# Norm weights applied by feature after the transposes, the stream transposed unweighted, scatter products split in two, first products in other PSUM banks

## The chip, the cores and the metric

The kernel runs on one core of a Trainium2 chip. The metric is device time in microseconds (us) of one execution. Five engines work side by side, each through its own instructions in a fixed order: PE (TensorE, matrix products and transposes), DVE (VectorE), ACT (ScalarE), POOL (GpSimd) and SP, which here only issues DMAs. An instruction that waits for another engine holds up everything behind it on its own engine. Before the change the kernel takes 1525.91 us, the median of three runs (1525.18 to 1528.49).

## The reference

256 tokens of 1024 features run through two blocks. Cut to what matters here, every sublayer reads a normalised copy of the stream `h` and adds its result back; in the second block the result is normalised too:

```
def rms_norm(x, gain):
    y = x * rsqrt(mean(x * x, axis=-1) + EPS)
    return y * gain

mem_n = rms_norm(mem, mem_norm)
h = x
h = h + hybrid_mixer(rms_norm(h, mix_norm), ...)
h = h + memory_cross_attention(rms_norm(h, cross_norm), mem_n, ...)
h = h + hierarchical_moe(rms_norm(h, moe_norm), ...)
h = rms_norm(h, final_norm)
for i in range(2):
    g = norm_g[i]
    h = h + 0.5 * rms_norm(swiglu(rms_norm(h, g[0]), ...), g[1])
    m = diff_attention(rms_norm(h, g[2]), ...) if i == 0 else neighborhood_attention(rms_norm(h, g[2]), ...)
    h = h + rms_norm(m, g[3])
    h = h + 0.5 * rms_norm(swiglu(rms_norm(h, g[4]), ...), g[5])
```

A weight (gain) is a vector over the 1024 features. The mixture of experts picks two of 16 experts for each token.

## The kernel before

The stream is two tiles `h0`, `h1` of 128 tokens by 1024 features. The stages are hybrid, cross, moe, ffn, differential, ffn, ffn, neighborhood, ffn. Each matrix product keeps fp32 precision by splitting both operands into a high and a low part (`wh`, `wl` for weights; `xt` high and low for the stream, features on partitions) and summing three matmuls per product (`mm3`, lines 332 to 334). The stream's copy has eight feature blocks, k0 to k7, of 128 features by 128 tokens for each tile; a product of 24 matmuls runs over k0 to k7 in that order.

The norm is taken apart: the gain is multiplied into the rows before the product, and the factor 1/rms of each token (`x.r`, `xr` in the trace) is applied to the product afterwards. The factors come from a chain of small POOL instructions (`rstd1`, line 179), which starts from sums of squares that ACT makes (`sumsq`, line 213).

The change sits in the passage from one stage to the next, `finish` and `leave`. At the end of a stage the results of tile 0 and tile 1 lie in four accumulator banks of PSUM (`acc`). For each tile `leave` makes the sums of squares, the POOL factor `f`, `yg` (the result times its post-norm gain) and then h += f*yg. To have the next stage's input early, it works out the weighted copy `hg` by itself: hg = h*g before the results are there (line 264), the product of both gains (265), `ygg` (281) and hg += f*ygg (286); h itself follows (290). The copy is transposed by PE, four blocks into one bank (`transpose_half`, line 226), and split into high (ACT, line 137) and low (DVE, line 138) parts, one instruction of 128x512 each. Tile 0 is transposed inside the last products of the stage; tile 1 is left to `x.second`, which the next stage calls after its first two products of tile 0. At the start of the program (memory and hybrid) there is no `hg`: the rows are transposed and a DVE multiply (line 231) applies the gain, then the two parts are made.

In PSUM, products and transposes take banks from a pool of four (`bank`); the four `acc` banks are a second pool. A product whose bank has not been read yet keeps the bank: in an ffn the first products are read by a silu (line 397) that needs `xr`, and by a DVE multiply (line 399), whose result is transposed (line 403).

In the mixture of experts the tokens of a pair of experts are gathered, multiplied (`gate_up`, line 1553), turned (line 1566, four transposes), multiplied again (`down`, line 1577) and scattered back by eight matmuls (line 1588), which for one pair stand between the next pair's gate_up and its transposes. Four broadcasts of a gain row over the partitions (`spread`, lines 1387 and 1388) are mixed in.

PE's order is the order in which the code is written. The order on DVE, ACT, POOL and SP is chosen by the framework's scheduler when the program is built.

Of the kernel before, what the change touches and what calls it, by code (L numbers as in the profile page):

```python
# [17 lines left out]
D = 1024  # L18
NT = 2
# [6 lines left out]
LAM_INIT = 0.8 - 0.6  # L26
GUESS = float(0x5F3759DF - (1 << 22))
# [15 lines left out]
class X:  # L43


    def __init__(self, net, apart=False):
        self.net = net
        if apart:
            self.p = [pool.tile([128, KT, NT * 128], F32R, tag=tag, name="xt", bufs=1) for pool, tag in ((net.mem, "m8"), (net.work, "t8"))]
        else:  # L50
            self.p = net.parts()
        self.third = lambda: None
        self.r, self.hg = net.small.tile([128, NT], F32, tag="xr", name="xr"), []
# [15 lines left out]
class Net:  # L69
    def __init__(self, ctx, tc, a):  # L70
# [3 lines left out]
        self.const = p("const", 1)  # L74
        self.wraw = p("wraw", 3)
# [9 lines left out]
        nc.vector.memset(self.ones, 1.0)  # L85

# [3 lines left out]
    def bank(self, shape):  # L90
        return self.ps_mm.tile([128] + shape, F32, tag="mm", name="bank")

# [13 lines left out]
    def gain(self, nxt):  # L106

        return self.bcast(nxt) if nxt.shape[0] == 1 else nxt
# [62 lines left out]
    def rstd1(self, sums, scale=1.0, out=None, late=None, by=None, eng=None):  # L171
# [10 lines left out]
        if late is not None:  # L182
            pre = self.small.tile([128, 1], F32, tag="pre", name="pre")
            op(pre, late, late, 0.5 / D, add=OP.mult)
# [14 lines left out]
    def norms_both(self, x, hs, after=None):  # L199
        ss = self.small.tile([128, NT], F32, tag="ssb", name="ssb")  # L200
# [19 lines left out]
    def transpose_half(self, xn, x, t, half, gain=None):  # L220
# [13 lines left out]
    def enter(self, x, t, h, g):  # L234

        hg = self.base.tile([128, D], F32, tag="xn", name="hg")
        x.hg.append(hg)
        for cs in HALVES:  # L240
            self.nc.vector.tensor_tensor(out=hg[:, cs], in0=h[:, cs], in1=g[:, cs], op=OP.mult)
        return lambda: self.turn(hg, x, t)

    def turn(self, hg, x, t, gain=None):
        for c in range(2):
            self.transpose_half(hg, x.p, t, c, gain)
# [5 lines left out]
    def leave(self, hs, ys, post, g, late, at):  # L252
# [5 lines left out]
        if x is not None:  # L258
            hg = x.hg = [self.base.tile([128, D], F32, tag="xn", name="hg") for _ in range(NT)]
        if post is not None:  # L260
            gain, scale, by = post
            if x is not None:
                for t in range(NT):
                    nc.vector.tensor_tensor(out=hg[t], in0=hs[t], in1=g, op=OP.mult)
                nc.vector.tensor_tensor(out=g, in0=gain, in1=g, op=OP.mult)

        def close(t):

            h, y = hs[t], ys[t]
            if post is None:  # L270
                for c, cs in enumerate(HALVES):
                    nc.vector.tensor_tensor(out=h[:, cs], in0=h[:, cs], in1=y[c], op=OP.add)
                    if x is not None:
                        self.entered = nc.vector.tensor_tensor(out=hg[t][:, cs], in0=h[:, cs], in1=g[:, cs], op=OP.mult)
                return lambda: None
# [8 lines left out]
            if x is not None:  # L284
                for cs in HALVES:
                    last = self.entered = nc.vector.scalar_tensor_tensor(out=hg[t][:, cs], in0=made[0][:, cs], scalar=f, in1=hg[t][:, cs], op0=OP.mult, op1=OP.add)

            def rest():
                for cs in HALVES:
                    ins = nc.vector.scalar_tensor_tensor(out=h[:, cs], in0=made[-1][:, cs], scalar=f, in1=h[:, cs], op0=OP.mult, op1=OP.add)  # L290
                    if last is not None:
                        self.after(ins, last)
            return rest

        def out(t, rest):
            rest()
# [6 lines left out]
        rest = close(0)  # L303
        for n, piece in enumerate(late):
            for c in range(2):
                if x is not None and at[c] == n:
                    self.transpose_half(hg[0], x.p, 0, c)
            piece()
        if x is None:
            out(0, rest)  # L310
            out(1, close(1))
            return
        last = close(1)
        if post is None and not self.moe_next:
            self.left, self.chunks = self.entered, 0
        out(0, rest)

        def second():
            self.turn(hg[1], x, 1)
            out(1, last)  # L320
# [38 lines left out]
    def ffn(self, x, hs, i, which, nxt):  # L359
# [3 lines left out]
        ys = self.acc()  # L363
# [25 lines left out]
        def first(m, t):  # L389
            load(m)  # L390
            ps = self.bank([256])
# [14 lines left out]
            if pending:  # L406
                pending.pop()()
# [9 lines left out]
        rows = x.rows()  # L417
        g1 = self.bcast(self.a["norm_g"][i, 1 if which == 1 else 5:][0:1])
        g2 = self.gain(nxt)
        for m in range(lead, MF):  # L420
# [9 lines left out]
            if pending:  # L430
                pending.pop()()
# [1331 lines left out]
```

## Time and profile before

| | |
|---|---|
| runs, median (lowest to highest) | 1525.91 us (1525.18 to 1528.49) |
| profiled execution, time | 1523.38 us |
| its span (first to last instruction) | 1521.5 us |
| PE busy | 1431.9 us, 94% of the span |
| DVE busy | 927.2 us, 61% |
| ACT busy | 730.8 us, 48% |
| POOL busy | 178.5 us, 12% |
| share of PE in the chain that ended last | 67% |
| mean granted TensorE clock | 0.982 |

The profile is one execution. "Busy" is the time in which an engine had an instruction at work; PE's 94% leave some 90 us idle in all, so that a change of the kernel's time has to come from there, from PE's own work or from the clock. The page's clock row shows tenths of full speed.

### The profile page before, as it was taken

Reading aid. Unit: us, or ns where it says so; the run is one execution under the profiler, and the core shown is the slowest. Engines: PE = TensorE matmul, PEld = TensorE weight load, DVE = VectorE, ACT = ScalarE, POOL = GpSimd, SP = SyncE. Lnnn points to the kernel's source line nnn. Section 1 sums busy time; section 2 is a strip of 40 time slices with the busy share of each in tenths; the row PEclk is TensorE's granted clock in tenths of the full one; section 3 lists DMA queues with packets and bytes.
Section 4 is the critical chain, followed back from the end, with each engine's and each line's share of the span. In section 5 each row is a group of like instructions: output and inputs, shape, how many; then the busy total and the mean of one; then the engine's idle time right before and its main releaser. Section 6 shows DMA issues by size and latency. Waiting matters only on the chain.

```text
span 1521.5 us, 22354 instructions
## 1 busy us (share of the span) xinstructions
PE 1431.9 (94%) x8412; PEld 1158.7 (76%) x8412; DVE 927.2 (61%) x1908; ACT 730.8 (48%) x1625; POOL 178.5 (12%) x446
## 2 busy tenths in 40 slices
PE   7999898799998999999988999999999999999997
PEld 6887774344445888879877888888888888788886
DVE  6786561111205866677668766676766777776665
ACT  6554441011114655556556555555555555565553
POOL 4222320000003100021014000040000400210000
PEclk9999998899999999999999999999999999999999
DMA  7453479979965755444334555536454355265540
GB/s 285 167 184 109 182 294 363 409 307 416 412 263 222 248 209 188 172 170 139 112 112 166 222 199 189 194 115 245 170 216 175 126 204 192 97 222 191 197 166 28
DMA packets 50630, 314.74 MB, mean 207 GB/s; under 512 B 6978, under 2 KB 7890, under 8 KB 15956
## 3 DMA queue, kind: packets, MB, share of 16 engines
q1 hardware_dynamic: 50516, 313.24, 55.4%
q8 instruction: 69, 1.13, 0.3%
q14 instruction: 45, 0.37, 0.1%
HBM read 312.15 MB, written 1.05 MB: 206 GB/s over the span
## 4 chain that ended last, share of the span: by engine, by line
PE 67%; POOL 4%; DVE 4%; ACT 3%; issue 2%; DVEq 0%; ACTq 0%; POOLq 0%
PE bank L344 19%; PE bank L347 9%; PE bank L1553 6%; PE acc L334 5%; PE acc L332 5%; PE acc L333 5%; PE bank L332 3%; PE bank L333 3%; PE bank L334 3%; PE bank L1577 3%; POOL rs_t L179 1%; PE bank L1509 1%; ACT pr L693 1%; DVE wl L129 1%; ACT junk L213 1%
## 5 line engine op out<-in xcount | busy, mean ns | idle before, releaser
L129 DVE TENSOR_TENSOR wl<-raw,wh 128x512 fp32r<-128x512 f32 x754 | 484.6, 693 | 29.8 <-ACT wh L128 29.3
L128 ACT ACTIVATE wh<-raw 128x512 fp32r<-128x512 f32 x754 | 419.9, 622 | 67.5 <-issue 24.4
L344 PE MATMUL bank<-xt,wh 128*128 128x512 f32 x1216 | 428.1, 397 | 0.0
L347 PE MATMUL bank<-xt,wl 128*128 128x256 f32 x1216 | 316.5, 281 | 0.0
L344 PEld LDWEIGHTS bank<-xt,wh 128*128 128x128 f32 x1216 | 222.9, 188 | 43.6
L347 PEld LDWEIGHTS bank<-xt,wl 128*128 128x128 f32 x1216 | 229.7, 189 | 13.8
L332 PE MATMUL bank<-wh,xt 128*128 128x256 f32 (+1 forms) x528 | 162.6, 308 | 9.7 <-ACT dT L674 4.2
L333 PE MATMUL bank<-wl,xt 128*128 128x256 f32 (+1 forms) x528 | 159.0, 301 | 2.6 <-DVE wl L129 2.3
L334 PE MATMUL bank<-wh,xt 128*128 128x256 f32 (+1 forms) x528 | 158.7, 301 | 1.5 <-DVE xt L138 1.5
L355 ACT ACTIVATE lo<-bank 128x256 f32<-128x256 f32 x152 | 58.4, 384 | 175.4 <-PE bank L344 175.3
L332 PE MATMUL acc<-wh,uh 128*128 128x512 f32 x352 | 137.5, 391 | 0.0
L334 PE MATMUL acc<-wh,ul 128*128 128x512 f32 x352 | 137.4, 390 | 0.0
L333 PE MATMUL acc<-wl,uh 128*128 128x512 f32 x352 | 137.0, 389 | 0.0
L332 PEld LDWEIGHTS bank<-wh,xt 128*128 128x128 f32 x528 | 104.7, 198 | 15.7 <-ACT dT L674 4.6
L1553 PE MATMUL bank<-chunk,gT 128*64 128x512 f32 x512 | 115.2, 603 | 0.0
L333 PEld LDWEIGHTS bank<-wl,xt 128*128 128x128 f32 x528 | 104.8, 198 | 5.8 <-DVE wl L129 4.0
L334 PEld LDWEIGHTS bank<-wh,xt 128*128 128x128 f32 x528 | 104.7, 198 | 4.6 <-DVE xt L138 2.5
L356 DVE TENSOR_TENSOR u<-bank,lo 128x256 f32<-128x256 f32 x76 | 32.3, 424 | 122.8 <-ACT lo L355 122.8
L1553 PEld LDWEIGHTS bank<-chunk,gT 128*64 128x64 f32 x512 | 41.5, 139 | 67.3 <-issue 66.6
L332 PE MATMUL bank<-xt,wh 128*128 128x256 f32 x296 | 85.6, 289 | 0.0
L333 PE MATMUL bank<-xt,wh 128*128 128x256 f32 x296 | 84.0, 284 | 0.0
L334 PE MATMUL bank<-xt,wl 128*128 128x256 f32 x296 | 83.9, 284 | 0.0
(340 smaller groups left out, 1987.4 us busy)
## 6 DMA issues: line engine op xcount, KB each, us to landing
raw<-in_gu_dram SPq DMA_DIRECT2D x88, 1024.0 KB, 4.8
raw<-in_wd_dram SPq DMA_DIRECT2D x44, 1024.0 KB, 4.9
chunk<-in_eg_dram SPq DMA_DIRECT2D x29, 1024.0 KB, 10.3
chunk<-in_eu_dram SPq DMA_DIRECT2D x28, 1024.0 KB, 10.9
chunk<-in_ed_dram SPq DMA_DIRECT2D x26, 1024.0 KB, 8.9
raw<-in_diff_qk_dram SPq DMA_DIRECT2D x8, 1024.0 KB, 4.8
raw<-in_na_qk_dram SPq DMA_DIRECT2D x8, 1024.0 KB, 4.9
raw<-in_mix_tm_dram SPq DMA_DIRECT2D x6, 1024.0 KB, 4.9
```

Source lines behind the costliest of these rows:

```text
L128: nc.scalar.activation(out=hi[:, q], in_=raw[:, q], func=AF.Copy)
L129: last = nc.vector.tensor_tensor(out=lo[:, q], in0=raw[:, q], in1=hi[:, q].bitcast(F32), op=OP.subtract)
L179: return eng.tensor_scalar(out=o, in0=i, scalar1=by, scalar2=to, op0=mul, op1=add)
L332: nc.tensor.matmul(out, lhsT=w[0], rhs=x[0], start=first, stop=False)
L333: nc.tensor.matmul(out, lhsT=w[0], rhs=x[1], start=False, stop=False)
L334: nc.tensor.matmul(out, lhsT=w[1], rhs=x[0], start=False, stop=last)
L344: nc.tensor.matmul(b, lhsT=w[0][:, k, j, :], rhs=x.p.both[:, :, k, :], start=k == 0, stop=k == KT - 1)
L347: nc.tensor.matmul(b[:, 0], lhsT=w[1][:, k, j, :], rhs=x.p[0][:, k, :], start=False, stop=False)
L355: self.nc.scalar.activation(out=lo, in_=b[:, 1], func=AF.Copy)
L356: self.nc.vector.tensor_tensor(out=out, in0=b[:, 0], in1=lo, op=OP.add)
L1553: nc.tensor.matmul(b[S * j:S * j + S], lhsT=g[:, 4 * c + k, j, :], rhs=wt, start=c + k == 0, stop=c + k == 4)
L1577: nc.tensor.matmul(b[i][S * j:S * j + S], lhsT=u[:, 2 * c + k, S * j:S * j + S], rhs=wt[:, i * 512:(i + 1) * 512], start=c + k == 0, stop= ...
```

## The change

Four edits in one.

1. All eleven gains lie in one constant tile, 128 features by 11 by 8 blocks (`gain_cols`), loaded by one DMA at the start. `hg` and `ygg` are gone. `h` is transposed, and each 128x128 block gets its gain while it leaves PSUM: ACT's copy takes the gain as its scale for the high part, and a DVE scalar_tensor_tensor makes the low part. So a tile takes eight small instructions on ACT and eight on DVE where it took two and two.
2. The first products of tile 0 (in ffn, differential and neighborhood) take banks of the `acc` pool (`early`); in an ffn two results may wait for their transposes instead of one.
3. The eight scatter matmuls are split into four, the turn's transposes, and four more.
4. `spread` broadcasts one gain row, in two pieces, instead of two rows in four; the broadcast DMAs of the next stage's gain rows are gone.

The diff, cut:

```diff
@@ transpose_half
-        q, s = slice(half * 4, half * 4 + 4), slice(t * 128, (t + 1) * 128)
-        if gain is not None:
-            raw = tp
-            tp = self.base.tile([128, 4, 128], F32, tag="xn", name="xn")
-            nc.vector.tensor_tensor(out=tp, in0=raw, in1=gain[:, q, None].to_broadcast([128, 4, 128]), op=OP.mult)
-        self.split(x[0][:, q, s], x[1][:, q, s], tp)
+        s = slice(t * 128, (t + 1) * 128)
+        for j in range(4):
+            k = half * 4 + j
+            by = gain[:, k:k + 1]
+            nc.scalar.activation(out=x[0][:, k, s], in_=tp[:, j, :], func=AF.Copy, scale=by)
+            nc.vector.scalar_tensor_tensor(out=x[1][:, k, s], in0=tp[:, j, :], scalar=by, in1=x[0][:, k, s].bitcast(F32), op0=OP.mult, op1=OP.subtract)
@@ leave
-        if x is not None:
-            hg = x.hg = [self.base.tile([128, D], F32, tag="xn", name="hg") for _ in range(NT)]
-        if post is not None:
-            gain, scale, by = post
-            if x is not None:
-                for t in range(NT):
-                    nc.vector.tensor_tensor(out=hg[t], in0=hs[t], in1=g, op=OP.mult)
-                nc.vector.tensor_tensor(out=g, in0=gain, in1=g, op=OP.mult)
...
-            made = []
-            for by_, tag in [(g, "ygg"), (gain, "yg")] if x is not None else [(gain, "yg")]:
-                v = w.tile([128, D], F32, tag=tag, name=tag, bufs=1)
-                for c, cs in enumerate(HALVES):
-                    nc.vector.tensor_tensor(out=v[:, cs], in0=y[c], in1=by_[:, cs], op=OP.mult)
-                made.append(v)
-            last = None
-            if x is not None:
-                for cs in HALVES:
-                    last = self.entered = nc.vector.scalar_tensor_tensor(out=hg[t][:, cs], in0=made[0][:, cs], scalar=f, in1=hg[t][:, cs], op0=OP.mult, op1=OP.add)
...
+            yg = w.tile([128, D], F32, tag="yg", name="yg", bufs=1)
+            for c, cs in enumerate(HALVES):
+                nc.vector.tensor_tensor(out=yg[:, cs], in0=y[c], in1=gain[:, cs], op=OP.mult)
+            for cs in HALVES:
+                nc.vector.scalar_tensor_tensor(out=h[:, cs], in0=yg[:, cs], scalar=f, in1=h[:, cs], op0=OP.mult, op1=OP.add)
...
-                    self.transpose_half(hg[0], x.p, 0, c)
+                    self.transpose_half(hs[0], x.p, 0, c, g)
...
-            self.turn(hg[1], x, 1)
-            out(1, last)
+            self.turn(hs[1], x, 1, g)
+            out(1)
@@ ffn, first
-            ps = self.bank([256])
+            ps = (self.bank if t else self.early)([256])
...
-            if pending:
-                pending.pop()()
+            if len(pending) == 2:
+                pending.pop(0)()
             pending.append(turn)
@@ moe, spread
-            if j <= follows:
-                ps = self.bank([512])
-                nc.tensor.matmul(ps, lhsT=self.ones[0:1, :], rhs=gains[j][0:1, cs], start=True, stop=True)
-                nc.scalar.activation(out=gains[j][:, cs], in_=ps, func=AF.Copy)
+            ps = self.bank([512])
+            nc.tensor.matmul(ps, lhsT=self.ones[0:1, :], rhs=gains[0][0:1, cs], start=True, stop=True)
+            nc.scalar.activation(out=gains[0][:, cs], in_=ps, func=AF.Copy)
@@ experts
-            if p != 2 and p:
-                scatter(p - 1)
-            turn(p)
+            for t in range(NT):
+                if p != 2 and p:
+                    scatter(p - 1, [t])
+                if not t:
+                    turn(p)
```

How the instructions stand now is shown at two places. The first is the passage from differential to ffn, which has the same pattern as the four other passages with a post-norm. This is DVE before: `ygg`, `yg`, `hg` and `h` are the updates of tile 0 and then tile 1, `xt<-bank,xt` is the low part of tile 0's transposed blocks, four at a time, and a wait on a name like Pool_49 is a wait for that engine.

```order
L286 SCALAR_TENSOR_TENSOR hg<-ygg,rs_r,hg 128x512 [waits DVE_49,Pool_49]
L286 SCALAR_TENSOR_TENSOR hg<-ygg,rs_r,hg 128x512 [waits DVE_49]
L290 SCALAR_TENSOR_TENSOR h_7255<-yg,rs_r,h_7255 128x512
L281 TENSOR_TENSOR ygg<-acc,gain 128x512 [waits DVE_49,Activation_49]
L138 TENSOR_TENSOR xt<-bank,xt 128x4x128 [waits Activation_49]
L290 SCALAR_TENSOR_TENSOR h_7255<-yg,rs_r,h_7255 128x512
L138 TENSOR_TENSOR xt<-bank,xt 128x4x128 [waits Activation_49]
L281 TENSOR_TENSOR ygg<-acc,gain 128x512
L281 TENSOR_TENSOR yg<-acc,gain 128x512 [waits DVE_49]
L281 TENSOR_TENSOR yg<-acc,gain 128x512
L286 SCALAR_TENSOR_TENSOR hg<-ygg,rs_r,hg 128x512 [waits Pool_49]
L286 SCALAR_TENSOR_TENSOR hg<-ygg,rs_r,hg 128x512 [waits DVE_49]
```

This is DVE now, at the same place: `h_7314` is tile 0, `h_7316` tile 1, and `xt<-bank,gain_cols,xt` the low part of one block of tile 0.

```order
L269 SCALAR_TENSOR_TENSOR h_7314<-yg,rs_r,h_7314 128x512 [waits DVE_49,Pool_49]
L269 SCALAR_TENSOR_TENSOR h_7314<-yg,rs_r,h_7314 128x512 [waits DVE_49]
L267 TENSOR_TENSOR yg<-acc,gain 128x512 [waits DVE_49,Activation_49]
L239 SCALAR_TENSOR_TENSOR xt<-bank,gain_cols,xt 128x128 [waits Activation_49] x2
L267 TENSOR_TENSOR yg<-acc,gain 128x512 [waits Activation_49]
L239 SCALAR_TENSOR_TENSOR xt<-bank,gain_cols,xt 128x128 [waits Activation_49] x2
L269 SCALAR_TENSOR_TENSOR h_7316<-yg,rs_r,h_7316 128x512 [waits DVE_49,Pool_49]
L239 SCALAR_TENSOR_TENSOR xt<-bank,gain_cols,xt 128x128 [waits Activation_49] x2
L269 SCALAR_TENSOR_TENSOR h_7316<-yg,rs_r,h_7316 128x512 [waits DVE_49]
L136 TENSOR_TENSOR wl<-raw,wh 128x512 [waits DMAHW5_49,Activation_49]
L239 SCALAR_TENSOR_TENSOR xt<-bank,gain_cols,xt 128x128 [waits Activation_49]
L136 TENSOR_TENSOR wl<-raw,wh 128x512
```

Before, both low parts of tile 0 stood ahead of the first instruction that waits for tile 1's factor (the last row but one, a wait for POOL). Now four of its eight blocks stand behind that instruction (the first row with `h_7316`), the last of them behind the rows shown and behind two more `wl`.

On ACT at the same place the squares of the stream (`junk,ss<-h`) of tile 1 have moved. Before:

```order
L137 ACTIVATE xt<-bank 128x4x128 [waits PE_49]
L213 ACTIVATE junk,ss<-acc 128x512 [waits PE_49,Activation_49]
L137 ACTIVATE xt<-bank 128x4x128 [waits PE_49]
L128 ACTIVATE wh<-raw 128x512 [waits DMAHW2_49]
L213 ACTIVATE junk,ss<-h_7255 128x1024 [waits DVE_49,Activation_49]
L128 ACTIVATE wh<-raw 128x512 x3
L397 ACTIVATE silu<-bank,xr 128x128 [waits PE_49,Pool_49]
L397 ACTIVATE silu<-bank,xr 128x128 [waits PE_49]
L213 ACTIVATE junk,ss<-h_7257 128x1024 [waits DVE_49,Activation_49]
```

Now:

```order
L238 ACTIVATE xt<-bank,gain_cols 128x128 [waits PE_49]
L220 ACTIVATE junk,ss<-h_7314 128x1024 [waits Activation_49]
L238 ACTIVATE xt<-bank,gain_cols 128x128 [waits DVE_49] x2
L135 ACTIVATE wh<-raw 128x512 [waits DMAHW5_49]
L135 ACTIVATE wh<-raw 128x512
L238 ACTIVATE xt<-bank,gain_cols 128x128 [waits DVE_49]
L135 ACTIVATE wh<-raw 128x512
L220 ACTIVATE junk,ss<-h_7316 128x1024 [waits DVE_49,Activation_49]
L238 ACTIVATE xt<-bank,gain_cols 128x128 [waits DVE_49]
```

The high part of a block waits for DVE's low part of the block before it in the same bank, and the last block (the last row) stands behind the squares of tile 1, which wait for tile 1's update on DVE.

The second place is PE in the mixture of experts, at the second pair: gate_up is `bank<-chunk,gT`, the turn `bank<-ident,silu`, down `bank<-chunk,uT`, scatter `acc<-y,ohT`. Before:

```order
L1553 MATMUL bank<-chunk,gT 64x512 x32
L1588 MATMUL acc<-y,ohT 128x512 x8
L1566 MATMUL bank<-ident,silu 128x128 x4
L1577 MATMUL bank<-chunk,uT 64x512 x16
L1588 MATMUL acc<-y,ohT 128x512 x8
```

Now:

```order
L1522 MATMUL bank<-chunk,gT 64x512 x32
L1557 MATMUL acc<-y,ohT 128x512 x4
L1535 MATMUL bank<-ident,silu 128x128 x4
L1557 MATMUL acc<-y,ohT 128x512 x4
L1546 MATMUL bank<-chunk,uT 64x512 x16
L1557 MATMUL acc<-y,ohT 128x512 x8
```

Four scatter matmuls have moved from ahead of the turn's transposes to behind them, ahead of the down product.

## Rows read from the trace of the kernel before

**Rows 1.** Windows at two passages: us, then busy us (instructions) by engine, clock, DMA share.

```profile
806.00:826.00 20.00, 15.89 (x115) 14.23 (x114) 16.52 (x30) 11.07 (x25) 12.79 (x31) 1.00 0.37 113
998.00:1018.00 20.00, 16.21 (x107) 14.83 (x106) 15.15 (x25) 8.90 (x20) 12.78 (x31) 0.91 0.19 71
```

**Rows 2.** PE's timeline, differential to ffn: start, us, engine, line, operation [idle before, released by].

```profile
820.56 0.33 PE L403 MATMUL bank<-ident,u 128*128 128x128 f32 x1 [2.96 <-DVE u L399]
821.52 0.36 PE L332 MATMUL bank<-wh,xt 128*128 128x256 f32 x1
821.72 0.28 PE L333 MATMUL bank<-wl,xt 128*128 128x256 f32 x1
821.84 0.28 PE L334 MATMUL bank<-wh,xt 128*128 128x256 f32 x1
```

**Rows 3.** PE's timeline, the same wait in the four other passages with a post-norm.

```profile
684.41 0.36 PE L332 MATMUL bank<-wh,xt 128*128 128x256 f32 x1 [2.25 <-DVE ropecs L664]
...
1012.42 0.33 PE L403 MATMUL bank<-ident,u 128*128 128x128 f32 x1 [2.84 <-DVE u L399]
...
1206.19 0.38 PE L332 MATMUL bank<-wh,xt 128*128 128x256 f32 x1 [2.69 <-ACT v L520]
...
1332.58 0.33 PE L403 MATMUL bank<-ident,u 128*128 128x128 f32 x1 [3.31 <-DVE u L399]
```

**Rows 4.** POOL's timeline, the instruction that ends tile 1's factor, in the five passages.

```profile
678.26 0.34 POOL L179 TENSOR_SCALAR rs_r<-rs_r,rs_q,xr 128x1 f32<-128x1 f32 x1
...
814.33 0.28 POOL L179 TENSOR_SCALAR rs_r<-rs_r,rs_q 128x1 f32<-128x1 f32 x1
...
1006.54 0.34 POOL L179 TENSOR_SCALAR rs_r<-rs_r,rs_q,xr 128x1 f32<-128x1 f32 x1
...
1199.62 0.34 POOL L179 TENSOR_SCALAR rs_r<-rs_r,rs_q,xr 128x1 f32<-128x1 f32 x1
...
1326.15 0.29 POOL L179 TENSOR_SCALAR rs_r<-rs_r,rs_q 128x1 f32<-128x1 f32 x1
```

**Rows 5.** Instructions by line and form: duration in ns (min/median/max), first and last start.

```profile
L137 ACT ACTIVATE xt<-bank x46: 365/597/617, 139.3 to 1334.0; 128x512 fp32r<-128x512 f32 x34, 128x256 fp32r<-128x256 f32 x12
L137 ACT ACTIVATE uh<-bank x24: 267/271/297, 489.1 to 1352.6; 128x128 fp32r<-128x128 f32 x24
...
L138 DVE TENSOR_TENSOR ul<-bank,uh x24: 275/283/284, 489.5 to 1353.1; 128x128 fp32r<-128x128 f32 x24
...
L290 DVE SCALAR_TENSOR_TENSOR h<-yg,rs_r,h x24: 737/744/752, 673.1 to 1517.6; 128x512 f32<-128x512 f32 x24
...
L213 ACT ACTIVATE junk<-h x20: 1042/1059/1076, 19.7 to 1332.3; 128x1024 f32<-128x1024 f32 x20
...
L129 DVE TENSOR_TENSOR wl<-raw,wh x754: 669/684/1792, 9.6 to 1488.9; 128x512 fp32r<-128x512 f32 x189
```

**Rows 6.** PE idle ahead of down (line 1577), by what ended it: us, times.

```profile
  ACT uT L823: 2.7, 4
  DVE uT L825: 2.4, 3
```

**Rows 7.** PE's timeline at one broadcast of a gain piece.

```profile
421.68 1.12 PE L1387 MATMUL bank<-gain,ones 1*128 1x512 f32 x2
422.73 0.65 PE L1553 MATMUL bank<-chunk,gT 128*64 128x512 f32 x2
```

**Rows 8.** The start: the memory's factors on POOL, the first product's scaling on PE.

```profile
19.10 0.20 POOL L151 TENSOR_TENSOR xr<-rs_r,rs_q 128x2 f32<-128x2 f32 x1
...
29.79 0.61 PE L63 MATMUL bank<-diag,ones 128*128 128x128 f32 x4
```

**Rows 9.** DVE's timeline, hybrid to cross.

```profile
180.74 0.17 DVE L1273 TENSOR_SCALAR rorder<-iota 128x4 f32<-128x4 f32 x1 [3.79 <-DMA iota<-in_c_iota_dram]
```

**Rows 10.** PE's timeline, moe to ffn.

```profile
481.78 0.58 PE L333 MATMUL bank<-wl,xt 128*128 128x256 f32 x1 [1.48 <-DVE wl L129]
...
502.19 0.33 PE L403 MATMUL bank<-ident,u 128*128 128x128 f32 x1 [1.20 <-DVE u L399]
```

More of the change, by code (lines that the diff above doesn't have):

```diff
@@ L52, in __init__ @@
         self.third = lambda: None
-        self.r, self.hg = net.small.tile([128, NT], F32, tag="xr", name="xr"), []
+        self.r = net.small.tile([128, NT], F32, tag="xr", name="xr")
     def rows(self):
@@ L91, in bank, with early @@
         return self.ps_mm.tile([128] + shape, F32, tag="mm", name="bank")
+    def early(self, shape):
+        return self.ps_acc.tile([128] + shape, F32, tag="acc", name="early")
     def wide(self, shape=[512]):
@@ L485, in one @@
                 w[c] = self.weights(chunks[c])
-            put(c, t, self.by_tokens(x, w[c], t))
+            put(c, t, self.by_tokens(x, w[c], t, t == 0 and c < lead))
         for t in range(NT):
@@ L832, in memory @@
             nc.sync.dma_start(out=mem[0][:, cs], in_=a["mem"][0:128, cs])
-            if cs.start == 0:
-                self.first_cols = self.work.tile([128, 2, KT], F32, tag="first", name="cols", bufs=1)
-                nc.sync.dma_start(out=self.first_cols, in_=a["first_cols"].rearrange("p (n k) -> p n k", n=2))
         raw, w, rows = [self.raw(a["xv"][0], 4)], {}, []
@@ L838, in memory @@
         raw.append(self.raw(a["xv"][1]))
-        x.turn = [lambda t=t: self.turn(mem[t], x, t, self.first_cols[:, 0]) for t in range(NT)]
+        x.turn = [lambda t=t: self.turn(mem[t], x, t, self.gain("mem_norm")) for t in range(NT)]
         def split(c):
@@ L1401, in again @@
                 nc.vector.tensor_tensor(out=hs[t], in0=x.h[0][:, t, :].bitcast(F32), in1=x.h[1][:, t, :].bitcast(F32), op=OP.add)
-        self.experts(ys, x.h, gr, pos, fetch, others, again, [lambda j=j, cs=cs: spread(j, cs) for j in range(2) for cs in HALVES])
-        g1, g2 = gains[0], gains[-1]
+        self.experts(ys, x.h, gr, pos, fetch, others, again, [lambda cs=cs: spread(cs) for cs in HALVES])
+        g1 = gains[0]
         x = X(self) if follows else None
+        if x is not None:
+            both = self.small.tile([128, KT], F32, tag="both", name="both", bufs=1)
+            nc.vector.tensor_tensor(out=both, in0=self.gain("final_norm"), in1=nxt, op=OP.mult)
         def add(t):
@@ L1581, in down, with scatter @@
             st["y", p] = y
-        def scatter(p):
+        def scatter(p, ts=range(NT)):
             ot = st["o", p]
-            for t in range(NT):
+            for t in ts:
                 for c in range(2):
@@ L1633, in emit @@
         if x_ is None:
-            x_, gain = X(net, s[0] == "moe"), None if s[0] == "hybrid" else net.bcast(g(*s[1]))
+            x_ = X(net)
             for t in range(NT):
                 nc.sync.dma_start(out=hs[t], in_=x[t * 128:(t + 1) * 128, :])
-            if s[0] == "hybrid":
-                x_.first, x_.second = (lambda t=t, v=x_: net.turn(hs[t], v, t, net.first_cols[:, 1]) for t in range(NT))
-            else:
-                net.enter(x_, 0, hs[0], gain)()
-                x_.second = net.enter(x_, 1, hs[1], gain)
-                net.norms_both(x_, hs)
+            x_.first, x_.second = (lambda t=t, v=x_: net.turn(hs[t], v, t, net.gain(s[1])) for t in range(NT))
         x_ = getattr(net, s[0])(x_, hs, *s[2:], nxt)
@@ L1743 @@
 STAGES = [
-    ("hybrid", None), ("cross", ("cross_norm",)), ("moe", ("moe_norm",)),
-    ("ffn", ("norm_g", (0, 0)), 0, 1), ("differential", ("norm_g", (0, 2))), ("ffn", ("norm_g", (0, 4)), 0, 2),
-    ("ffn", ("norm_g", (1, 0)), 1, 1), ("neighborhood", ("norm_g", (1, 2))), ("ffn", ("norm_g", (1, 4)), 1, 2),
+    ("hybrid", "mix_norm"), ("cross", "cross_norm"), ("moe", "moe_norm"),
+    ("ffn", (0, 0), 0, 1), ("differential", (0, 2)), ("ffn", (0, 4), 0, 2),
+    ("ffn", (1, 0), 1, 1), ("neighborhood", (1, 2)), ("ffn", (1, 4), 1, 2),
 ]
```

115 lines of the change are left out of this document (48 added, 67 removed).

## The prediction

> **What bounds the kernel now.** I read the page first, then PE's timeline for its idle stretches, then who ended each of them. PE is busy in all but some 90 us, so the steady parts of every stage are PE's own work and the edits hardly touch them. What the change can win or lose lies in four kinds of places: the start, the passages between stages, the turn in the experts, and the granted clock after a stall. The five passages with a post-norm look alike. PE runs two products of tile 0, then sits idle for 2.25 to 3.31 us, 14.05 us in all, until something that reads a bank is done: `u` or `ropecs` or `v` [rows 2, 3]. Each of these needs `xr`, since a full bank is read with it; the banks are the wait. Tile 1's factor f1 comes from POOL at 678.60, 814.61, 1006.88, 1199.96 and 1326.44 us [rows 4], so some 6 us before that idle time ends. In the order of before nothing that the two products need is behind f1; in the order after, half of it is.
>
> **The five passages.** Removed on DVE: the weighted copy, the gain products, `ygg`. Removed on PE: the wait for `xr`, since early banks let the third product of tile 0 start without it. By that alone 14.05 us go. What is late next is tile 0's own input. Each block is now an ACT and a DVE instruction, and within a bank the next block's ACT waits for the last block's DVE, so the eight blocks are two chains in step. The scheduler has put tile 1's update, which waits for f1, ahead of four of the eight low parts on DVE, and on ACT the squares of tile 1 (which wait for that update) ahead of the last high part. So the first product, having done k0 to k2, waits for f1 and then for this row of work. On DVE: update 0.74, two low parts 2 x 0.28, update 0.74, then `wl` 0.68, low part 0.28, two `wl` 1.37, last low part 0.28, in all 4.65 [rows 5]. On ACT, where no `wl` stands between: 0.74 + 0.57 + 0.74, squares 1.06, high part 0.27, low part 0.28, in all 3.66 [rows 5]. Neither form of the block is in the trace: ACT with a per-feature scale and DVE's scalar_tensor_tensor at 128x128 are taken at 0.271 and 0.283, the nearest rows of that size from PSUM (a 128x512 took 0.597). Consecutive instructions overlap a little, so I take 3.8 between the two ends. Then come the last three matmuls, 0.36; the second product, 24 at 0.12 = 2.9; and the eight transposes of tile 1, 0.85 (0.96 from the turn's transpose to the third product, with nine transposes in it) [rows 2]. The third product starts at f1 + 7.9 (from 7.7 with 3.66 to 8.7 with 4.65).
>
> That is 686.5, 822.5, 1014.8, 1207.9 and 1334.3, against 684.41, 821.52, 1013.38, 1206.19 and 1333.54 before (with 0.96 added where the row is that of the turn) [rows 2 to 4]: later by 2.1, 1.0, 1.4, 1.7 and 0.8, together **+7.0** (+6 to +11). Below that only an earlier f1 leads, since DVE has less to do and POOL's chain ran slower beside a busy DVE: 1 us of it is worth 5. Tile 1's own eight blocks are hidden by the third product and the first products' `silu` wait no bank; if that cover fails it costs some 0.5 us each.
>
> The Trainium skill, "VectorE: DVE Perf Modes", section "The TRN2 errata — SBUF-src ops pay a fixed extra latency per instruction", speaks against the edit: a cost per instruction is paid again by each small tile, and it advises operands of 512 elements or more. The rows agree, 4 x 0.271 against 0.597 [rows 5]. Its table would put a 128-element low part from PSUM at (120 + 128)/0.96 = 258 ns, an estimate; the sum would then be +6.5 instead of +7.0.
>
> **The clock.** The passage at 998 us had 0.91 of full speed, the one at 806 us 1.00 [rows 1]; each lists 20 us, so a fall costs about 1.8 us. After the change PE's idle time comes in one place, 3.8 us and more rather than 2.3 to 3.3, so a fall is likelier in each passage. I take one and a half more: **+2.7** (0 to +6).
>
> **The start.** The gain multiply goes, but memory's tile 1 lands late and decides. ACT's order puts the squares of the memory behind high parts of tile 1, and the last of those high parts behind the first `kv`, which waits for memory's `xr`. That came at 19.30 [rows 8] and will come 1 to 2 us later; the last block follows `kv` and two `wh`, so memory's first products end about 3 us later. The squares of the stream move back too, so the scaling product that stood at 29.79 [rows 8] starts near 33 to 34. **+4** (0 to +6; below nothing not, as memory's second tile is the same DMA).
>
> **Hybrid to cross.** DVE waits for a DMA until 180.74 [rows 9]. In the order after, that instruction still stands ahead of most low parts, which are now a chain of small ones: **+2** (0 to +3). Cross to moe has POOL's chain at its end before and after: 0.
>
> **Experts.** Down waited 2.7 + 2.4 us for `uT` [rows 6]. Four scatter matmuls now stand in that wait, about 1.1 us of PE work against gaps of 0.7 to 0.8. The four that stay ahead of the turn just cover the time until its input is made; if they don't, some of it comes back. **-4.9** (0 to -5.1). Of four broadcasts, each 1.05 us of PE [rows 7], two go: **-2.1**.
>
> **Moe to ffn.** DVE loses four multiplies, the turn no longer stands ahead of a product. Idle times of 1.48 and 1.20 [rows 10] shrink: **-2.5** (0 to -2.7).
>
> The broadcast loads of gain rows lay beside other work and free nothing on PE: 0. One 128x88 load ahead of the memory's: 0 to +0.3, in the start's range.
>
> **Sum.** 7.0 + 2.7 + 4 + 2 - 4.9 - 2.1 - 2.5 = +6.2 on the profiled execution, 1523.38 to 1529.6. It lies 2.5 under the median of the runs, so the runs should have 1525.91 + 6.2 = **1532**.
>
> **Rivals.**
> 1. *The early banks pay in full.* If f1 comes about 3 us sooner, or the low parts behind it are no longer needed by the time PE gets there, the five waits go (-14.05), two falls of the clock with them (-3.6), the experts and moe to ffn give 9.5 and the start costs 4, hybrid to cross 1: -22, **1504**. For it: the waits are real and the banks end them. Against it: f1 rests on squares of tile 1's last product, which end no sooner. It decides from the point where f1 + 3.8 is earlier than the end of two products without a stall. This is the other side of my forecast.
> 2. *About even passages.* f1 two us sooner: passages -3, no fall of the clock, start +1, hybrid to cross 0.5, the rest -9.5: -11, **1515**. For it: DVE has less to do around each passage, and POOL's chains may stretch where DVE is busy.
> 3. *All goes wrong together at the passages.* The full DVE row (4.65), the clock falling in all five, start +6: 9 + 5.4 + 6 + 3 - 7 = +16, **1542**. For it: a stall of more than 4 us in one place. Against it: four falls of the clock in longer stalls are a guess from two.
> 4. *No change*: the losses at start and passages and the gains in the experts cancel, **1526**; this is the low end of the forecast's range, and has no mechanism of its own.
>
> **How the numbers follow.** Forecast 0.53, rival 1 0.13, rival 2 0.17, rival 3 0.17. About 3 us (0.2%) is what a measurement of this kernel can tell from no change. Faster: rivals 1 and 2, 0.30. Same: 0.12, all from the forecast's lower end. Slower: the rest of the forecast and rival 3, 0.58. The forecast's own range is 1526 to 1539, from the bounds above. The range for 8 in 10 takes in rival 2 and rival 3's middle: 1511 to 1543.
>
> **What would show it.** In the profile after, in each of the five passages: PE idle inside the first product at k3 and at k7, released by the DVE low part or the ACT high part; DVE's update of tile 1 waiting for POOL between low parts of tile 0; no wait ahead of the third product. In the experts: no idle time ahead of down. At the start: the scaling product after 32 us. It is wrong if the first product of a passage runs without a stall, if f1 comes 2 us sooner after the last product of tile 1, or if down still waits.

## The result, and the profile after

The changed kernel takes 1535.56 us, the median of five runs (1534.37 to 1537.56), against 1525.91 us (1523.78 to 1528.49, five runs too) of the kernel before. The ratio is 1.0063, with a 95% interval of 1.0049 to 1.0078: 9.65 us slower. The profiled execution took 1537.56 us, its span 1535.8 us, at a mean granted clock of 0.966 (before 0.982). It is the slowest of its five runs, and that of before (1523.38) lies under all five of its own; the two are 14.2 us apart, so the stage by stage sizes below add up to 14.3 and not to 9.65.

PE sat idle less than before: its span less its busy time is 80.4 us (before 89.6). But its busy time rose from 1431.9 to 1455.4 us, with nearly the same matmuls (8408, before 8412), as the clock was at the lower of its two levels for some 50 us more (worked out from the two mean clocks).

Here is the passage from differential to ffn that [rows 2] show of before. PE's timeline after the change (start, duration, instruction, idle time before it and who ended it): the three rows of the first product that waited, then tile 1's transposes and the first matmul of the third product.

```profile
817.10 0.39 PE L310 MATMUL early<-wh,xt 128*128 128x256 f32 x1 [0.22 <-DVE xt L239]
817.93 0.39 PE L308 MATMUL early<-wh,xt 128*128 128x256 f32 x1 [0.44 <-ACT xt L238]
820.16 0.58 PE L310 MATMUL early<-wh,xt 128*128 128x256 f32 x1 [1.73 <-DVE xt L239]
827.60 1.03 PE L233 MATMUL bank<-ident,h 128*128 128x128 f32 x8
828.39 0.36 PE L308 MATMUL early<-wh,xt 128*128 128x256 f32 x1
```

The first product now waits within itself, for low and high parts of blocks, at k2 and k3; the wait of 2.96 us ahead of the third product is gone. DVE at the same time:

```profile
816.70 0.60 DVE L239 SCALAR_TENSOR_TENSOR xt<-bank,gain_cols,xt 128x128 fp32r<-128x128 f32 x2
819.09 0.75 DVE L269 SCALAR_TENSOR_TENSOR h<-yg,rs_r,h 128x512 f32<-128x512 f32 x1 [1.79 <-POOL rs_r L186]
819.76 0.60 DVE L239 SCALAR_TENSOR_TENSOR xt<-bank,gain_cols,xt 128x128 fp32r<-128x128 f32 x2
820.28 0.74 DVE L269 SCALAR_TENSOR_TENSOR h<-yg,rs_r,h 128x512 f32<-128x512 f32 x1
820.94 0.68 DVE L136 TENSOR_TENSOR wl<-raw,wh 128x512 fp32r<-128x512 f32 x1
821.54 0.35 DVE L239 SCALAR_TENSOR_TENSOR xt<-bank,gain_cols,xt 128x128 fp32r<-128x128 f32 x1
821.80 1.28 DVE L136 TENSOR_TENSOR wl<-raw,wh 128x512 fp32r<-128x512 f32 x2
823.01 0.34 DVE L239 SCALAR_TENSOR_TENSOR xt<-bank,gain_cols,xt 128x128 fp32r<-128x128 f32 x1
```

Tile 1's update waits 1.79 us for POOL's factor with four of tile 0's low parts behind it. The last low part ends at 823.35. ACT is at the squares of tile 1 until 822.3 before the last high part:

```profile
821.19 1.05 ACT L220 ACTIVATE junk<-h 128x1024 f32<-128x1024 f32 x1
822.13 0.19 ACT L220 ACTIVATION_READ_ACCUMULATOR junk<-h 128x1 f32 x1
822.23 0.36 ACT L238 ACTIVATE xt<-bank,gain_cols 128x128 fp32r<-128x128 f32 x1
```

POOL's factor of tile 1 and tile 0's `xr`, as in [rows 4]:

```profile
818.77 0.28 POOL L186 TENSOR_SCALAR rs_r<-rs_r,rs_q 128x1 f32<-128x1 f32 x1
...
825.34 0.28 POOL L186 TENSOR_SCALAR xr<-rs_r,rs_q 128x1 f32<-128x1 f32 x1
```

From the factor (819.05) to the last low part it is 4.3 us, and to the third product 9.3 us. With the last matmuls, the second product and the transposes at full speed it would be 4.3 + 0.36 + 2.9 + 0.85 = 8.4; the rest is the clock. Windows as in [rows 1] (the number after POOL's instructions is the granted clock), and the stretch in between:

```profile
806.00:826.00 20.00, 16.79 (x77) 13.63 (x76) 13.17 (x25) 11.61 (x30) 11.32 (x27) 0.83 0.40 139
998.00:1018.00 20.00, 16.66 (x78) 13.57 (x77) 11.68 (x24) 10.43 (x27) 9.27 (x27) 0.89 0.33 121
819.10:825.90 6.80, 5.74 (x23) 5.21 (x24) 5.46 (x11) 3.53 (x9) 5.97 (x9) 0.50 0.16 41
```

For 6.8 us, from 819.1 on, the clock was at the lower of its two levels (1.2 GHz; the upper is 2.4). It fell within a stretch, 816.4 to 820.2, in which PE started only five matmuls. The four other passages look the same:

```profile
679.10:685.90 6.80, 5.69 (x25) 5.48 (x26) 3.52 (x15) 2.28 (x6) 5.27 (x17) 0.50 0.10 30
1013.70:1020.50 6.80, 5.93 (x26) 5.73 (x27) 5.32 (x12) 5.22 (x12) 5.75 (x12) 0.50 0.02 5
1208.20:1215.00 6.80, 6.20 (x27) 6.00 (x28) 2.08 (x6) 2.24 (x5) 5.35 (x17) 0.50 0.36 133
1337.90:1344.70 6.80, 6.33 (x26) 5.80 (x27) 5.15 (x12) 4.04 (x10) 5.85 (x11) 0.50 0.22 55
```

The blocks' own durations, which the trace of before could not show (ns, min/median/max):

```profile
L238 ACT ACTIVATE xt<-bank,gain_cols x144: 347/368/461, 6.2 to 1352.9; 128x128 fp32r<-128x128 f32 x144
...
L239 DVE SCALAR_TENSOR_TENSOR xt<-bank,gain_cols,xt x144: 337/344/353, 6.6 to 1353.3; 128x128 fp32r<-128x128 f32 x144
```

In the experts the idle time ahead of down [rows 6] went from 5.1 us to this:

```profile
  ACT uT L798: 1.4, 2
```

The start: PE's first product of the stream, and the product that was at 29.79 [rows 8].

```profile
28.19 0.58 PE L308 MATMUL bank<-wh,xt 128*128 128x256 f32 x1 [3.85 <-DVE xt L239]
...
36.60 0.61 PE L64 MATMUL bank<-diag,ones 128*128 128x128 f32 x4
```

From cross to moe, the instruction that takes the router's product for tile 1 (`rlt`, on DVE) waited before for POOL's `xr`, and now for PE's product. Before, then after:

```profile
228.93 0.24 DVE L1287 SCALAR_TENSOR_TENSOR rlt<-bank,xr,rbias 128x20 f32<-128x20 f32 x1 [1.27 <-POOL xr L179]
...
241.63 0.24 DVE L1258 SCALAR_TENSOR_TENSOR rlt<-bank,xr,rbias 128x20 f32<-128x20 f32 x1 [2.00 <-PE bank L1256]
```

How far the changed kernel falls behind from one like instruction of PE to the next, in the two traces:

| stretch | from and to (before) | change, us | forecast, us |
|---|---|---|---|
| start, to the hybrid's attention | 0 to 143.8 | +6.8 | +4 |
| hybrid to the transposes after cross | 143.8 to 216.8 | +3.5 | +2 |
| cross to moe, to the first gate_up | 216.8 to 238.9 | +2.6 | 0 |
| experts | 238.9 to 475.3 | -11.1 | -7.0 |
| moe to ffn | 475.3 to 505.8 | -1.4 | -2.5 |
| ffn, to tile 0's transposes | 505.8 to 672.7 | 0.0 | 0 |
| five passages, each to the next (the last to the end) | 672.7 to 1521.5 | +3.9, +2.1, +1.2, +3.1, +3.5 | +7.0 and +2.7 for the clock |

### The profile page after: what moved, and what is told of

Its sections match the earlier page's. It is cut to its first block, busy times and chain, and to the rows that moved or that the text cites. A ratio compares the mean times of both kernels' runs of the same rounds, so it can differ in the third digit from the quotient of the medians.

```text
span 1535.8 us, 22480 instructions
## 1 busy us (share of the span) xinstructions
PE 1455.4 (95%) x8408; PEld 1179.3 (77%) x8408; DVE 896.6 (58%) x1953; ACT 756.6 (49%) x1743; POOL 161.6 (11%) x446
## 4 chain that ended last, share of the span: by engine, by line
PE 67%; POOL 4%; DVE 3%; ACT 3%; issue 2%; DMA 1%; DVEq 0%; ACTq 0%; POOLq 0%
PE bank L320 18%; PE bank L323 9%; PE acc L308 6%; PE acc L309 6%; PE acc L310 6%; PE bank L1522 5%; PE bank L308 3%; PE bank L310 2%; PE bank L309 2%; PE bank L1546 2%; POOL rs_t L186 1%; PE early L310 1%; PE bank L1478 1%; DMA raw<-in_gu_dram 1%; ACT junk L220 1%
## 5 line engine op out<-in xcount | busy, mean ns | idle before, releaser
L308 PE MATMUL bank<-wh,xt 128*128 128x256 f32 (+1 forms) x392 | 123.4, 315 | 9.5 <-ACT dT L649 4.4
L310 PE MATMUL bank<-wh,xt 128*128 128x256 f32 (+1 forms) x392 | 119.9, 306 | 1.4 <-DVE xt L239 1.4
L309 PE MATMUL bank<-wl,xt 128*128 128x256 f32 (+1 forms) x392 | 119.3, 304 | 0.0
L308 PEld LDWEIGHTS bank<-wh,xt 128*128 128x128 f32 x392 | 78.4, 200 | 15.7 <-ACT dT L649 4.9
L308 PE MATMUL bank<-xt,wh 128*128 128x256 f32 x296 | 87.0, 294 | 0.5 <-ACT xt L238 0.5
L309 PE MATMUL bank<-xt,wh 128*128 128x256 f32 x296 | 85.7, 289 | 0.0
L310 PEld LDWEIGHTS bank<-wh,xt 128*128 128x128 f32 x392 | 78.3, 200 | 4.2 <-DVE xt L239 2.0
L309 PEld LDWEIGHTS bank<-wl,xt 128*128 128x128 f32 x392 | 78.4, 200 | 1.8
```

The source lines that it names most:

```text
L308: nc.tensor.matmul(out, lhsT=w[0], rhs=x[0], start=first, stop=False)
L309: nc.tensor.matmul(out, lhsT=w[0], rhs=x[1], start=False, stop=False)
L310: nc.tensor.matmul(out, lhsT=w[1], rhs=x[0], start=False, stop=last)
```

## The experiments

Each kernel has its ratio to the kernel before on the same chip; between experiments these ratios are compared, not the times. 0.1% is 1.5 us.

**Tile 0's blocks first (e1).** Two orderings are added to the changed kernel.

```diff
                 ins = nc.vector.scalar_tensor_tensor(out=h[:, cs], ...)
+                if t and x is not None:
+                    self.after(ins, self.low)
...
             out(1)
+            if post is not None:
+                self.after(self.squared, high)
```

> The changed kernel with two added orderings in the five passages with a post-norm: tile 1's update of h on DVE stands behind the last low part of tile 0, and the squares of tile 1 on ACT behind tile 0's last high part. Theory A (the order makes the stall: tile 1's factor is waited for ahead of half of tile 0's blocks): the first product runs without waiting for POOL, the third starts some 3 us after tile 1's factor instead of 9.3. The fourth is then held by the silu that waits for xr ahead of tile 1's blocks, so about 3 us a passage are won, and some of the clock's falls go: 1535.6 - 16 = about 1520 (1514 to 1524). Theory B (the size makes it: eight small pairs chained through a bank are slow wherever they stand): 1532 to 1536.

Measured 1524.08 us, ratio 0.9991 (0.9979 to 1.0002): some 11 us under the changed kernel, as fast as before, at the slow end of what theory A gave. In its trace no fall of the clock is left in the five passages; it is the trace of the fastest of its twelve runs (granted clock 0.980; the median of the twelve is 0.9765), so others may have had some. PE, same passage:

```profile
808.27 0.36 PE L313 MATMUL early<-wh,xt 128*128 128x256 f32 x1
...
814.19 0.28 PE L313 MATMUL early<-wh,xt 128*128 128x256 f32 x1
...
817.05 1.04 PE L233 MATMUL bank<-ident,h 128*128 128x128 f32 x8
...
820.81 0.36 PE L313 MATMUL bank<-wh,xt 128*128 128x256 f32 x1
...
822.30 0.38 PE L313 MATMUL bank<-wh,xt 128*128 128x256 f32 x1 [0.41 <-ACT xt L238]
...
826.59 0.27 PE L383 MATMUL bank<-ident,u 128*128 128x128 f32 x1
```

And ACT:

```profile
817.74 0.37 ACT L377 ACTIVATE silu<-early,xr 128x128 f32<-128x128 f32 x1 [4.22 <-POOL xr L186]
...
820.34 0.62 ACT L238 ACTIVATE xt<-bank,gain_cols 128x128 fp32r<-128x128 f32 x2
```

The order was the larger part of the passages' loss: shown (in the two traces, 12.8 us from the first passage on). What is left is in two products. The first (808.27 to 814.19, where the second begins) still takes 5.9 us instead of 2.9, held by its small blocks one after the other; so the third product starts 5.0 us after tile 1's factor (812.85) and not 3. And the fourth (820.81), tile 1's first, takes 5.8 us instead of 2.9, since its blocks start on ACT at 820.34, behind a `silu` that waited for `xr`.

**Early banks alone (e2)**, on the kernel before: `ps = (self.bank if t else self.early)([256])` and its like for the other two stages, and two pending turns.

> The kernel before with nothing but the early banks for the first products of tile 0 and two pending turns. Theory A: the wait of 2.3 to 3.3 us ahead of the third product goes in all five passages, since hg's blocks are ready before tile 1's factor; part of it comes back at the first product of tile 1, whose blocks stand on ACT behind the silu that waits for xr: 5 to 14 us faster than before, about 1517. Rival: the banks were not the wait, what stands behind takes all of it: 1526, as before.

Measured 1519.94 us, ratio 0.9964 (0.9951 to 0.9977): 5.5 us faster, at the lower end. Five waits of 14 us in all were taken away, and 5.5 came of it. In its trace there are other waits instead: inside the third product for the low part of a weight (`wl`), in two passages, and inside tile 1's first product for its blocks. The longest, from differential to ffn:

```profile
818.72 0.58 PE L337 MATMUL early<-wl,xt 128*128 128x256 f32 x1 [2.99 <-DVE wl L133]
```

**Split scatter alone (e3)**, on the kernel before: the last hunk of the diff and nothing else.

> The kernel before with nothing but the split scatter. Theory: the idle time ahead of down (5.1 us in seven places) goes and nothing else changes: 1525.9 - 4.9 = 1521. Rival: four matmuls ahead of the turn do not cover the time until its input is made, the wait moves there: 1524 to 1526.

Measured 1520.53 us, ratio 0.9972 (0.9962 to 0.9982): 4.3 us by the ratio, 5.2 by the medians. The term of 4.9 stands.

**The start as before (e4)**, in the changed kernel.

```diff
+        if big:
+            q, raw = slice(half * 4, half * 4 + 4), tp
+            tp = self.base.tile([128, 4, 128], F32, tag="xn", name="xn")
+            nc.vector.tensor_tensor(out=tp, in0=raw, in1=gain[:, q, None].to_broadcast([128, 4, 128]), op=OP.mult)
+            self.split(x[0][:, q, s], x[1][:, q, s], tp)
+            return
...
```

> The changed kernel with the start as before: the gain by one DVE multiply of 128x512 into SBUF, then one high and one low part of 128x512, for memory and the first norm; all else as changed. In the traces the changed kernel is 6.8 us behind when the hybrid's attention begins. Theory: the small blocks and the order on ACT cost that, and it is carried to the end: 1529. Rival: it is taken up by a later wait (a DMA, the moe's load of a count): 1535.

Measured 1530.81 us, ratio 1.0033 (1.0021 to 1.0045): 4.6 us under the changed kernel. At the hybrid's attention the whole 6.8 us are back (143.4 us, against 150.6); some 2 us of it are taken up later, as the rival had it in part; 1.5 of them are the stop that the last section shows.

**The readers of the early banks behind tile 1's blocks (e5)**, on top of e1.

```diff
+                for ins, part in x.readers:
+                    self.after(ins, getattr(self, part))
...
```

> The kernel of the first experiment with one more ordering: what reads the early banks with xr (silu, rot, v and the rope products) stands behind tile 1's blocks on ACT and DVE. In the first experiment's trace the first product of tile 1 takes 5.8 us instead of 2.9 in the passage to the second ffn, with its blocks behind that silu. Theory: this is the rest of what the order costs, some 2 to 3 us in each of five passages: 1524.1 - 12 = 1512. Rival: POOL's xr or the blocks' own chain holds the product just as long: 1521 to 1524.

Measured 1527.12 us, ratio 1.0015 (1.0002 to 1.0028): 3.7 us slower than e1, where 12 less were expected; slower than the rival's 1521 to 1524 too. My theory of the rest fell. The fourth product no longer waits; the turn ahead of it does:

```profile
824.84 0.33 PE L388 MATMUL bank<-ident,u 128*128 128x128 f32 x1 [2.10 <-DVE u L384]
```

The transposes of tile 1 started at 818.84 here; its eight pairs, with weight parts between them, last to 825.2, and the `silu` that the turn needs now stands behind them. A wait was moved, not ended.

**e5 with the start as before (e6).**

> The kernel of the last experiment with the start of the fourth (the gain by one DVE multiply, parts of 128x512). The two touch different places, so their gains should add: 4.75 us under the last one, about 1507. Rival: the start's gain is taken up by a later wait: 1511.

Measured 1520.06 us, ratio 0.9977 (0.9964 to 0.9991): 5.8 us under e5. That the start's cost adds to the passages' held.

**Large blocks everywhere (e7)**: e6, with the form of e4 in all places.

> The kernel of the sixth experiment with all blocks in the forms of the start: per half one DVE multiply, one high part and one low part of 128x512 in place of four and four of 128x128, everywhere; the orderings kept. Theory A (the order did it, not the size): within 4 us of the sixth, on either side, since the first product may start some 1.4 us later but has no chain to wait for: 1503 to 1511. Theory B (the chain of small instructions is what costs): 10 us or more faster, under 1499.

Measured 1511.58 us, ratio 0.991 (0.9888 to 0.9933): 10.2 us under e6 by the ratios, 8.5 by the medians. With the same added orderings the form of the blocks is worth nearly as much as the order was, though it adds a DVE multiply per half. It is more than size: the parts are now made from a copy outside PSUM and no longer take a factor, and no run separates the three. Tile 1's parts now take from 814.8 to 818.2, and the wait at the turn is

```profile
817.59 0.30 PE L394 MATMUL bank<-ident,u 128*128 128x128 f32 x1 [0.98 <-DVE u L390]
```

This is 0.9% under the kernel before, the fastest here beside e11 below.

**Added work for PE in the stall (e8, e10)**: matmuls on operands that are there, into a bank that nobody reads.

```diff
+WARM = {3: 24, 6: 8, 7: 12}
...
             for k in range(KT):
+                if k in WARM:
+                    warm(WARM[k])
```

> The changed kernel with 44 more matmuls of 128x256 in the first product of each of the five passages (24 ahead of k3, 8 ahead of k6, 12 ahead of k7), on operands that are there, into a bank that nobody reads: work for PE in the stall. Theory: a good part of the passages' loss is the granted clock, which falls to half for 6.8 us in each after the stall while PE runs the next products; kept busy, it stays, and 1.4 to 2.4 us come back in each: 1524 to 1529. Rival: the stall itself is the whole loss, or the clock falls all the same: 1535 or more.

Measured 1536.03 us, ratio 1.0071 (1.0051 to 1.0091): no gain. The clock did stay at full speed through all five passages, but the matmuls ahead of k7 ended some 0.7 us after its block was there and gave the gain away. So with {3: 24, 6: 5, 7: 6}:

> The kernel of the eighth experiment with 35 added matmuls in place of 44 (24 ahead of k3, 5 ahead of k6, 6 ahead of k7), so that none stands in the way of a block: in the eighth the clock stayed at full speed through the passages, but the added matmuls ahead of k7 ended 0.7 us after its block was there. Theory: the fall of the clock costs about 1 us in each passage (the second product takes 4.0 us instead of 2.9): 1535.6 - 5 = 1530.5 (1528 to 1533). Rival: it costs nothing, since the passage waits for xr anyway: 1535 to 1536.

Measured 1531.55 us, ratio 1.0037 (1.0025 to 1.0049): 4 us under the changed kernel with more work on PE. In the two traces the way from tile 0's to tile 1's transposes is shorter by 6.8 us in the five passages together, and a part is lost again behind it. The windows of [rows 1] in this kernel:

```profile
806.00:826.00 20.00, 18.93 (x134) 17.06 (x134) 13.46 (x29) 11.88 (x30) 13.51 (x31) 1.00 0.45 141
998.00:1018.00 20.00, 19.00 (x126) 16.97 (x126) 11.75 (x24) 11.08 (x28) 11.63 (x30) 1.00 0.24 80
```

So the falls of the clock in the five passages cost some 4 us of the 9.65: shown, as a lower bound, since the added matmuls are in the way a little.

**e7 without the readers' ordering (e9).**

> The kernel of the seventh experiment (blocks of 128x512, start as before, tile 1's update and squares behind tile 0's blocks) without the ordering of the fifth, which moved its wait to the turn instead of ending it. If that ordering costs as much here as there (some 3 us between the first and the fifth, set against the kernel before): 1508 (1505 to 1511). If it costs nothing once the blocks are large: 1511 to 1513.

Measured 1525.1 us, ratio 1.0002 (0.9993 to 1.001). The expectation was wrong by its sign: the ordering that cost 3.7 us with small blocks is worth 14 with large ones. Without it DVE has this in the same passage:

```profile
813.40 3.25 DVE L136 TENSOR_TENSOR wl<-raw,wh 128x512 fp32r<-128x512 f32 x5
816.57 0.28 DVE L385 TENSOR_TENSOR u<-silu,early 128x128 f32<-128x128 f32 x1
816.76 1.28 DVE L238 TENSOR_TENSOR xn<-bank,gain_cols 128x512 f32<-128x512 f32 x2
```

and PE this:

```profile
818.17 0.58 PE L319 MATMUL bank<-wh,xt 128*128 128x256 f32 x1 [2.34 <-ACT xt L144]
```

Tile 1's multiply stands behind five weight parts and a `u`, the fourth product waits 2.3 to 2.6 us in the three passages to an ffn, and the clock falls in two. The spans of the two profiled executions differ by 9.4 us and the medians by 13.5: that of e9 (1521.64) is the fastest of its eleven runs, 3.5 us under their median, and that of e7 0.6 over.

**Early banks and split scatter together (e11)**, on the kernel before.

> The kernel before with the early banks and the split scatter, without the gains by feature. The two gained 5.7 and 5.2 us alone and touch different stages: 1525.2 - 10.9 = 1514 to 1515. Rival: they share a wait (a fall of the clock, a DMA): 1517 to 1520.

Measured 1515.12 us, ratio 0.9927 (0.991 to 0.9944), against 0.9964 x 0.9972 = 0.9936 for the two: they add.

**The changed kernel without early banks (e12).**

> The changed kernel without its early banks (and with one pending turn); all else as changed. Theory A: in the changed order the third product cannot start before xr is there anyway, so the banks pay nothing or little: 1535 to 1537. Rival: they pay what they paid in the kernel before: 1541.

Measured 1537.65 us, ratio 1.0085 (1.0072 to 1.0098): the banks pay 3.4 us by the ratio, 2.1 by the medians, where they paid 5.5 before. They lost about half of their worth; the expectation (1535 to 1537, nothing or little) was a little too low. In its trace the first product waits where it waits with them:

```profile
818.40 0.58 PE L310 MATMUL bank<-wh,xt 128*128 128x256 f32 x1 [1.72 <-DVE xt L239]
...
826.10 1.04 PE L233 MATMUL bank<-ident,h 128*128 128x128 f32 x8
```

## Why the prediction was right, and which sizes were off

The forecast was 1532 and slower; 1535.56 lies in the forecast's own range (1526 to 1539), and the mechanism is the one that was named.

- *The stall at tile 0's blocks.* Right in cause, and nearly in size: 4.3 us from the factor to the last low part, where 3.8 was taken between 3.66 and 4.65; DVE's row with the `wl` in it ended last, not ACT's. One sign did not show: PE has no idle time at k7, for at the lower clock it came there (822.63) only as the last high part was done (822.59). That f1 comes no sooner held too: 5.8 us after tile 0's first transposes in both kernels (819.05 less 813.23 now, 814.61 less 808.78 before).
- *The block's price* was too low: ACT 0.368 instead of 0.271, DVE 0.344 instead of 0.283. The nearest rows had no per-feature factor. The Trainium skill's table ("VectorE: DVE Perf Modes", section "The TRN2 errata — SBUF-src ops pay a fixed extra latency per instruction") made 0.258 of the DVE part, an estimate; the trace has 0.344, and the measurement decides. Its advice, operands of 512 elements or more, goes the way of e7, 8.5 to 10 us; but DVE's own time is no smaller there (two multiplies 1.28 and two low parts of 0.69 for a tile, against 2.16 for eight small low parts in a row at the start), so what e7 saved is more likely the waits in the chain than a cost per instruction, which no run separates.
- *The clock* was the term that was mis-sized most in the passages. A fall in one and a half more passages, at 1.8 us, was 2.7; it fell in all five, for 6.8 us each where the two falls in the passages before lasted 3.4. e10 puts at least 4 us on it. That it fell in each was the mechanism of rival 3; the result lies between the forecast and that rival.
- *The start* lost 6.8 us and not 4. My reason was half wrong: memory's `xr` came at 19.54 against 19.30, nearly as before, and PE was 1.75 us late and not 3 when it had waited for memory's last blocks (the stream's transposes start at 22.43, before at 20.68). The longer wait is that of the stream's own blocks, 16 and 16 small instructions with both squares among them: PE's first product of the stream begins at 28.19 instead of 23.9, 4.3 us, and it then runs at half speed, 2.5 us more.
- *Hybrid to cross* lost 3.5 where 2 was forecast, and only in part as forecast: at tile 1's first transposes, behind DVE's wait for the DMA, PE was 5.6 us behind (189.11 for 183.52), less than at the hybrid's attention. The loss comes after that. PE waits 2.03 us for tile 1's second update, which stands behind low parts; then its products wait for tile 1's small blocks and run at the lower clock, for 10.2 us from 191.0 on, where it was 3.4 before.
- *Cross to moe* lost 2.6 where nothing was forecast, because POOL's chain was to end last before and after. It ended last before (`rlt` waits for `xr`); after the change `xr` is there at 238.33, and the router's product for tile 1, held by tile 1's small blocks and the lower clock, ends 3 us later. This step of the prediction was wrong. The large blocks of e7 did not make either stretch clearly faster: there too `rlt` waits for the product.
- *Moe to ffn* gave 1.4 and not 2.5: the waits of 1.48 and 1.20 are gone, but there too the first products now wait for their small blocks, five times 0.2 to 0.6 us.
- *The experts.* The split scatter gave what was said (e3). The rest of the 11.1 is the two broadcasts, about 2.4 us at that place in the trace, and some 4 us that nobody forecast, 3 of them a stop of PE that is gone (last section).
- *The early banks* were said to pay 14 us by themselves with tile 0's input as the next wait. Alone they paid 5.5 (e2), because a weight's low part and tile 1's input are close behind; in the changed kernel 2 to 3.

That the total came so near is in part luck. In the two traces the terms outside the experts sum to +25.3 where 13.2 were forecast, 12 us too little, and the experts gave 4 more than forecast, most of it by that stop; and the pair of profiled executions lies farther apart than the medians do.

Taken together: without the gains by feature the other parts are worth 11.1 us (e11). The gains by feature cost that and 9.65 more, about 21 (with the two broadcasts left aside), of which the order on DVE and ACT explains 11 (with the falls of the clock that it causes) and the start 4.6; the rest goes with the form of the blocks, which e7 shows to be worth 8.5 to 10 at another order. No run shows that applying the gains by feature pays by itself: e7 (0.991), the best kernel that has it, is not clear of e11 (0.9927), which leaves it out.

## What to carry to other kernels

Before an instruction is split into small ones that a scheduler may place, look at what it can put between them: a chain of eight pairs lets in every wait that two large pairs kept out. Where a wait on PE is taken away, price the next two waits behind it as well; five of 2.3 to 3.3 us gave 1.1 each. And an ordering is worth what the sizes around it make of it: the same one cost 3.7 us and gave 14.

## What the hardware showed that was not expected

A stop in the experts that no change aimed at went away, and gave 3 us. In the kernel before PE stops in the middle of a group of sixteen matmuls, with nothing to wait for that the profile shows:

```profile
304.39 1.44 PE L1509 MATMUL bank<-one,xt 128*128 128x256 f32 x6 [3.00 <-issue]
```

In the changed kernel the group runs through:

```profile
312.04 3.75 PE L1478 MATMUL bank<-one,xt 128*128 128x256 f32 x16 [6.03 <-DVE one L1467]
```

The stop was 2.7 to 3.1 us in all four kernels whose start is that of before (the kernel before, e2, e3, e11), 1.5 to 2.2 in those with large blocks at the start (e4, e6, e7, e9), which come there 2.6 to 4.6 us later, and at most 0.4 in those that come there 9 us or more later (the changed kernel, e1, e5, e8, e10, e12). It takes up a part of what a faster start gives. But that the late start is the cause is not shown. The stop also stands at another place: ahead of the tenth matmul of the group in the first four, of the fourteenth or sixteenth in the next, and behind the group in the last; and where the place is the same, to come later did not shorten it (e11 comes 1.9 us later than e3 and stops 0.4 longer). What ends it isn't in the profile, and no run was made on it.

The clock fell to its lower level in all five passages, for 6.8 us each, where PE started only some five matmuls in 3.8 us in the middle of a product, and in none of them when 35 matmuls filled that time (e10).
